# One instruction per convolution tap for latents and context, and GpSimd's arithmetic beside it on VectorE

## The chip, the cores and the metric

The kernel runs on one core of a Trainium2 chip. The metric is the device time of one execution in microseconds (us). A core has TensorE (matrix products), VectorE and ScalarE (elementwise work), GpSimd (elementwise work, and here the queue that issues part of the weight loads) and SyncE (which here only issues DMA). In the profile they are PE, DVE, ACT, POOL and SP; PEld is TensorE's load of weights. Each engine works through its own queue in order. L372 is line 372 of the kernel.

## The reference, cut to what matters

The model is a block with two linear-attention branches (gated delta rule, "GDN", and gated linear attention, "GLA") over 256 latent tokens and 256 context tokens, a routed mixture of 32 experts, and a second block behind it. The change lies in the inputs of the GDN branch: queries, keys and values go through a depthwise 3x3 convolution and a SiLU. The latents are an image of 4 rows of 64 tokens; the context is one row of 256 tokens, which sees the middle row of the taps only.

```python
def conv_latent(t, conv_w):
    b, l, ch = t.shape
    rows = l // GRID_W                      # 256 // 64 = 4
    return depthwise_conv2d(t.reshape(b, rows, GRID_W, ch), conv_w).reshape(b, l, ch)

def conv_context(t, conv_w):
    mid = CONV_SIZE // 2
    return depthwise_conv2d(t[:, None], conv_w[mid:mid + 1])[:, 0]

qkv_lat = jax.nn.silu(conv_latent(p_lat[..., :3 * GDN_WIDTH], conv_w))
qkv_ctx = jax.nn.silu(conv_context(p_ctx[..., :3 * GDN_WIDTH], conv_w))
```

Behind it, per head and direction, a chunked recurrence is solved: a triangular solve inside each chunk, then a scan over the chunks with a state of 128x128.

## The kernel before

Eight heads are worked in four pairs (gdn, L650). A generator, gdn_pair, holds the three steps of one pair. Its first step (L395 to L460) loads six blocks of w_in of 512 KB through GpSimd's queue (L399). It splits each into a high and a low part for exact fp32 products (wsplit, L381, with split, L48: the high part is rounded on ScalarE at L49, the low part is the difference at L50, on VectorE or, for the value blocks of the first two pairs, on GpSimd). It projects with three products for each of 8 blocks (mm3, L75), convolves (conv_silu, L357), transposes keys and values, and takes the norms with a reciprocal root (L57 to L72). The second step (L461 to L492) forms the decay matrices e, mt, at and qg. The third (L495 to L534) writes blocks of mt to DRAM, reads them back one block per partition (X), solves 31 steps of a triangular system on VectorE (L515, L516), and spreads the result with DMAs into AB. Then gdn_levels combines the blocks and gdn_scan runs the chunks.

In gdn the first pair's three steps come first. For each pair then the first step of the next pair is written, then levels and scan of this pair, then the other two steps of the next, then fill work that doesn't depend on them: lat_act (projections of gates), mod_steps (a modulation row, w_mod loaded through SyncE's queue into the same ring of six tiles as w_in, L161; TensorE product L162; a sum on VectorE at L172) and parts of the GLA branch. From this text the framework's planner sets the order of each engine's queue at build time by its own costs and inserts all waits; no order is written out by hand. So instructions of one pair run between those of another.

The convolution works on the transposed projection: 128 channels on the partitions, 256 (queries, latents only) or 512 tokens (keys and values: 256 latents, then 256 context) along the free dimension. ScalarE copies the latents into a zero-bordered pad of 6 rows of 66 (L364), starts the sum acc with the middle tap over all tokens (L365), and copies the context into a second pad of 258 (L367). Each of the eight other taps is one VectorE instruction over 256 latents, acc = pad x tap + acc (L372), rows outside the image included, where the pad is zero. For the two middle-row taps that the context has besides, ScalarE forms the product (L374, tile cx, one buffer) and GpSimd adds it (L375). A tanh (L377) and a closing product (L378) make the SiLU. There are 24 convolutions, 8 of them for queries.

Behind gdn come gla, merge, the expert stage (moe), whose weights stream through SyncE's queue, and the second block (post).

Of the kernel before, what the change touches and what calls it, by code (L numbers as in the profile page):

```python
# [7 lines left out]
F32 = mybir.dt.float32  # L8
# [4 lines left out]
OP = mybir.AluOpType  # L13
# [217 lines left out]
def gates(K, dbg=None):  # L231
# [4 lines left out]
    K.gdn_es = ExitStack()  # L236
    padp = K.gdn_es.enter_context(tc.tile_pool(name="pads", reuse_waits="tile", bufs=1, side="right"))
    for i in range(2):
        pl_ = padp.tile([P, 6, 66], F32, name=f"padl{i}")
        pc_ = padp.tile([P, 258], F32, name=f"padc{i}")  # L240
        nc.vector.memset(pl_, 0.0)
        nc.vector.memset(pc_, 0.0)
        K.pads.append((pl_, pc_))
    K.npad = 0
    es = ExitStack()
    gp = es.enter_context(tc.tile_pool(name="gp", reuse_waits="tile", bufs=1, side="right"))
# [110 lines left out]
def conv_silu(K, src, n_tok, ct, out, eng):  # L357

    nc = K.nc
    pl, pc = K.pads[K.npad % 2]  # L360
    K.npad += 1
    acc = K.gpool.tile([P, 512], F32, name="acc", bufs=2)
    al = acc[:, 0:256].rearrange("p (r w) -> p r w", r=4)
    nc.scalar.activation(pl[:, 1:5, 1:65], src[:, 0:256].rearrange("p (r w) -> p r w", r=4), AF.Copy)  # L364
    nc.scalar.activation(acc[:, :n_tok], src, AF.Copy, scale=K.taps[:, 4 * 24 + ct:4 * 24 + ct + 1])  # L365
    if n_tok > 256:
        nc.scalar.activation(pc[:, 1:257], src[:, 256:512], AF.Copy)  # L367
    cx = K.gpool.tile([P, 256], F32, name="cx")
    for tap in (0, 1, 2, 3, 5, 6, 7, 8):
        dy, dx = tap // 3, tap % 3  # L370
        w = K.taps[:, tap * 24 + ct:tap * 24 + ct + 1]
        eng.scalar_tensor_tensor(al, pl[:, dy:dy + 4, dx:dx + 64], w, al, op0=OP.mult, op1=OP.add)  # L372
        if n_tok > 256 and dy == 1:
            nc.scalar.activation(cx, pc[:, dx:dx + 256], AF.Copy, scale=w)  # L374
            nc.gpsimd.tensor_add(acc[:, 256:512], acc[:, 256:512], cx)  # L375
    th = K.gpool.tile([P, 512], F32, name="th", bufs=2)
    nc.scalar.activation(th[:, :n_tok], acc[:, :n_tok], AF.Tanh, scale=0.5)  # L377
    eng.scalar_tensor_tensor(out, th[:, :n_tok], 1.0, acc[:, :n_tok], op0=OP.add, op1=OP.mult)  # L378
# [12 lines left out]
def gdn_pair(K, pr):  # L391
# [14 lines left out]
    for hh in range(2):  # L406
        h = pr * 2 + hh
        H = Ctx()
        heads.append(H)
        H.h = h  # L410
        H.qT = gp.tile([P, 256], F32, name="qT", bufs=2)
        H.kT = gp.tile([P, 512], F32, name="kT", bufs=4)
        vT = gp.tile([P, 512], F32, name="vT", bufs=1)
        for j, (dst, n) in enumerate(((H.qT, 256), (H.kT, 512), (vT, 512))):

            hi, lo = wsplit(K, ws[hh * 3 + j], P, nc.gpsimd if pr < 2 and j == 2 else None)
            ps = psum.tile([P, 512], F32, name="pj", bufs=2)
            for k in range(8):
                mm3(nc, ps[:, :n], hi[:, k, :], lo[:, k, :], K.hh[:, k, :n], K.hl[:, k, :n], k == 0, k == 7)
            conv_silu(K, ps[:, :n], n, j * 8 + h, dst, nc.vector)  # L420

        pk = K.G()
        for t in range(4):
            nc.tensor.transpose(pk[:, t * P:(t + 1) * P], H.kT[:, t * P:(t + 1) * P], K.ident)
        H.kt = gp.tile([P, 4, P], F32, name="kt", bufs=4)
        nc.scalar.activation(H.kt, pk.rearrange("p (t n) -> p t n", t=4), AF.Copy)
        ns = gp.tile([P, 6], F32, name="ns", bufs=2)
        sq = gp.tile([P, 512], F32, name="th", bufs=2)
        for t in range(4):
            nc.scalar.activation(sq[:, t * P:(t + 1) * P], H.kt[:, t, :], AF.Square, accum_out=ns[:, t:t + 1])  # L430
        pn = K.G()
        sq = gp.tile([P, 512], F32, name="th", bufs=2)
        nc.scalar.activation(sq[:, :2 * P], H.qT, AF.Square)
        for t in range(2):
            nc.tensor.matmul(pn[:, t:t + 1], sq[:, t * P:(t + 1) * P], K.ones[:, 0:1], start=(t == 0), stop=(t == 1),
                             skip_group_check=True)
        nc.vector.tensor_copy(ns[:, 4:6], pn[:, 0:2])
        nq = gp.tile([P, 6], F32, name="nq", bufs=2)
        nc.vector.tensor_scalar(nq, ns, 4 * EPS, None, op0=OP.add)
        r = gp.tile([P, 6], F32, name="r", bufs=2)  # L440
        rsqrt(K, gp, r, nq, 6)

        r2 = gp.tile([P, 6], F32, name="r2", bufs=2)
        nc.vector.tensor_mul(r2, r, r)
        H.d = gp.tile([P, 2, 4], F32, name="d", bufs=4)
        bh = K.beta.rearrange("p d c h -> p d c h")[:, :, :, h]
        nc.vector.tensor_mul(H.d, bh, r2[:, None, 0:4].to_broadcast([P, 2, 4]))
        hn = gp.tile([P, 4], F32, name="hn", bufs=2)
        nc.vector.scalar_tensor_tensor(hn, nq[:, 0:4], 0.5, r[:, 0:4], op0=OP.mult, op1=OP.mult)
        nc.vector.tensor_scalar(K.aq[:, :, h], nq[:, 4:6], 128.0 * EPS, None, op0=OP.mult)  # L450

        pv = K.G()
        for t in range(4):
            nc.tensor.transpose(pv[:, t * P:(t + 1) * P], vT[:, t * P:(t + 1) * P], K.ident)
        H.vs = gp.tile([P, 4, P], F32, name="vs", bufs=4)
        for t in range(4):
            nc.scalar.activation(H.vs[:, t, :], pv[:, t * P:(t + 1) * P], AF.Copy, scale=hn[:, t:t + 1])
        H.dk = gp.tile([P, 2, 4], F32, name="dk", bufs=4)
        nc.vector.tensor_mul(H.dk, H.d, K.kds.rearrange("p (d t h) -> p d t h", d=2, t=4)[:, :, :, h])
    yield heads  # L460
    for hh, H in enumerate(heads):  # L461
# [14 lines left out]
        for d in range(2):  # L476
            gbc = gp.tile([P, 4, P], F32, name="gbc", bufs=2)
            nc.scalar.dma_start(gbc, dap(K.gD, d * 32 * P + h * P, [[0, P], [8 * P, 4], [1, P]]))
            e = gp.tile([P, 4, P], F32, name="e", bufs=2)
            s = 1 if d == 0 else -1  # L480
            nc.gpsimd.affine_select(out=e, in_=gbc, pattern=[[0, 4], [s, P]], compare_op=OP.is_ge,
                                    fill=-1e30, base=0, channel_multiplier=-s)
            for t in range(4):
                col = d * 32 + t * 8 + h
                nc.scalar.activation(e[:, t, :], e[:, t, :], AF.Exp, bias=K.ngc[:, col:col + 1])
            for t in range(4):
                nc.vector.scalar_tensor_tensor(H.mt[:, d, t, :], pg[:, t * P:(t + 1) * P], H.d[:, d, t:t + 1],
                                               e[:, t, :], op0=OP.mult, op1=OP.mult)
            nc.vector.tensor_mul(H.at[:, d], pq[:, 0:256].rearrange("p (t i) -> p t i", t=2), e[:, 0:2, :])
            nc.scalar.activation(H.qg[:, d], gbc[:, 0:2, :], AF.Exp)  # L490
            nc.gpsimd.tensor_mul(H.qg[:, d], H.qg[:, d], H.qT.rearrange("p (t i) -> p t i", t=2))
    yield  # L492


# [1517 lines left out]
```

## Time and profile before

| | us |
|---|---|
| median of 3 runs | 2082.15 (2078.74 to 2091.74) |
| profiled execution, its own time | 2083.65 |
| its span, first to last instruction | 2081.9 |
| TensorE busy | 1898.8 |
| VectorE busy | 965.6 |
| ScalarE busy | 652.5 |
| GpSimd busy | 184.0 |

The profile is of one execution. Busy is time in which an engine works on an instruction; idle time has a releaser, the instruction or DMA whose end let the engine go on. Groups of instructions show how many there are (xN), their busy time, the mean duration of one in ns, and the idle time before them. Durations by line are min/median/max in ns. PEclk is TensorE's granted clock as a share of full speed. The convolutions run from 66 to 407 us of the span, the expert stage from about 745 to 1710 us.

### The profile page before, as it was taken

Reading aid. Unit: us, or ns where it says so; the run is one execution under the profiler, and the core shown is the slowest. Engines: PE = TensorE matmul, PEld = TensorE weight load, DVE = VectorE, ACT = ScalarE, POOL = GpSimd, SP = SyncE. Lnnn points to the kernel's source line nnn. Section 1 sums busy time; section 2 is a strip of 40 time slices with the busy share of each in tenths; the row PEclk is TensorE's granted clock in tenths of the full one; section 3 lists DMA queues with packets and bytes.
Section 4 is the critical chain, followed back from the end, with each engine's and each line's share of the span. In section 5 each row is a group of like instructions: output and inputs, shape, how many; then the busy total and the mean of one; then the engine's idle time right before and its main releaser. Section 6 shows DMA issues by size and latency. Waiting matters only on the chain. (4 is left out here: it accounts for less than half of the span.)

```text
span 2081.9 us, 27700 instructions
## 1 busy us (share of the span) xinstructions
PE 1898.8 (91%) x10742; PEld 1159.6 (56%) x10743; DVE 965.6 (46%) x2245; ACT 652.5 (31%) x1369; POOL 184.0 (9%) x247
## 2 busy tenths in 40 slices
PE   4796989799998999999999999999999889989998
PEld 1664768687986763333333333333333228779997
DVE  2797785857464641212122221221211137676777
ACT  2553545467554420000000000000000004555554
POOL 1343122211112000000000000000000000000000
PEclk8798999899999989999999999999999988998999
DMA  7347654437544689999999999999999994433551
GB/s 261 77 122 206 183 169 116 112 103 206 169 151 151 254 325 417 417 414 418 417 416 418 418 416 417 418 416 417 418 418 416 417 345 139 140 102 121 183 182 41
DMA packets 191939, 569.60 MB, mean 274 GB/s; under 512 B 47919, under 2 KB 90776, under 8 KB 158650
## 3 DMA queue, kind: packets, MB, share of 16 engines
q1 hardware_dynamic: 160064, 507.19, 63.1%
q0 software_dynamic: 13392, 47.72, 7.4%
q10 hardware_dynamic: 18346, 12.86, 2.5%
q8 instruction: 86, 1.41, 0.3%
q14 instruction: 51, 0.42, 0.1%
HBM read 555.22 MB, written 12.50 MB: 273 GB/s over the span
## 5 line engine op out<-in xcount | busy, mean ns | idle before, releaser
L50 DVE TENSOR_TENSOR wlo<-w,whi 128x1024 fp32r<-128x1024 f32 (+1 forms) x185 | 223.9, 1211 | 132.6 <-ACT whi L49 129.8
L1308 PE MATMUL pg<-w,xT 128*64 128x512 f32 x1024 | 274.4, 605 | 3.5 <-DMA w<-in_w_gu_dram 3.4
L1308 PE MATMUL pl<-w,xT 128*64 128x512 f32 x1024 | 268.1, 593 | 0.0
L49 ACT ACTIVATE whi<-w 128x1024 fp32r<-128x1024 f32 (+1 forms) x189 | 197.3, 1047 | 217.8 <-PE pj L77 70.4
L1330 PE MATMUL po<-w,aT 128*64 128x512 f32 x1024 | 239.9, 608 | 7.1 <-DMA w<-in_w_down_dram 5.7
L1230 ACT ACTIVATE th<-ga 128x512 f32<-128x512 f32 x32 | 20.2, 632 | 613.8 <-DVE ga L1228 613.8
L1338 DVE TENSOR_TENSOR o<-po,g 64x512 f32<-64x512 f32 x64 | 44.1, 689 | 260.1 <-PE po L1330 259.4
L1308 PEld LDWEIGHTS pl<-w,xT 128*64 128x64 f32 x1024 | 75.2, 137 | 146.4 <-issue 146.4
L1330 PEld LDWEIGHTS po<-w,aT 128*64 128x64 f32 x1024 | 69.5, 139 | 141.7 <-issue 121.9
L1308 PEld LDWEIGHTS pg<-w,xT 128*64 128x64 f32 x1024 | 65.2, 136 | 139.4 <-issue 115.9
L1228 DVE TENSOR_SCALAR ga<-pg 128x512 f32<-128x512 f32 x32 | 22.1, 691 | 244.8 <-PE pg L1308 244.8
L77 PE MATMUL pj<-wlo,hh 128*128 128x256 f32 x384 | 116.2, 303 | 2.8 <-DVE wlo L50 2.8
L76 PE MATMUL pj<-whi,hh 128*128 128x256 f32 x384 | 115.2, 300 | 2.9 <-ACT whi L49 2.9
L78 PE MATMUL pj<-whi,hl 128*128 128x256 f32 x384 | 114.6, 299 | 0.0
L76 PE MATMUL pj<-hh,whi 128*128 128x512 f32 (+1 forms) x264 | 100.9, 384 | 12.6 <-ACT hh L49 9.1
L372 DVE SCALAR_TENSOR_TENSOR acc<-padl,taps,acc 128x256 f32<-128x256 f32 x192 | 104.3, 557 | 10.1 <-ACT acc L365 8.0
L78 PE MATMUL pj<-hh,wlo 128*128 128x512 f32 (+1 forms) x264 | 100.0, 380 | 5.9 <-DVE wlo L50 5.7
L77 PE MATMUL pj<-hl,whi 128*128 128x512 f32 (+1 forms) x264 | 100.9, 382 | 0.1
L1288 POOL CAST se<-sel 128x128 fp32r<-128x128 f32 x32 | 22.4, 702 | 828.4 <-PE pl L1292 828.4
L1267 PEld LDWEIGHTS tr<-S,h 128*128 128x128 f32 x480 | 57.9, 191 | 48.6 <-issue 34.9
L77 PEld LDWEIGHTS pj<-wlo,hh 128*128 128x128 f32 x384 | 78.0, 203 | 11.0 <-DVE wlo L50 4.2
L1360 PE MATMUL y<-o,PwT 128*128 128x512 f32 (+1 forms) x136 | 72.2, 641 | 13.0 <-DVE o L1338 10.2
(682 smaller groups left out, 3601.7 us busy)
## 6 DMA issues: line engine op xcount, KB each, us to landing
w<-in_w_gu_dram SPq DMA_DIRECT2D x256, 1024.0 KB, 18.2
w<-in_w_down_dram SPq DMA_DIRECT2D x139, 1024.0 KB, 20.0
w<-in_w_in_dram POOLq DMA_DIRECT2D x72, 512.0 KB, 5.4
w<-in_w_mod_dram SPq DMA_DIRECT2D x48, 512.0 KB, 6.9
w<-in_w_up_dram SPq DMA_DIRECT2D x22, 1024.0 KB, 5.1
w<-in_w_in_dram SPq DMA_DIRECT2D x8, 1024.0 KB, 9.8
gbc<-gD ACTq DMA_DIRECT2D x16, 256.0 KB, 6.2
actD<-la ACTq DMA_DIRECT2D x16, 256.0 KB, 5.0
```

Of the source, the lines that this page charges most:

```text
L49: K.nc.scalar.activation(hi, src, AF.Copy)
L50: (lo_eng or K.nc.vector).tensor_sub(lo, src, hi)
L76: nc.tensor.matmul(out, ah, bh, start=first, stop=False, **kw)
L77: nc.tensor.matmul(out, ah, bl, start=False, stop=False, **kw)
L78: nc.tensor.matmul(out, al, bh, start=False, stop=last, **kw)
L372: eng.scalar_tensor_tensor(al, pl[:, dy:dy + 4, dx:dx + 64], w, al, op0=OP.mult, op1=OP.add)
L1267: nc.tensor.matmul(p[:, kk * P:kk * P + m * CAP], h2[:, t, k * P:(k + 1) * P], S[:, t, e0:e1].rearrange("p e c -> p (e c)"), start=(kk == ...
L1288: nc.gpsimd.tensor_copy(se, sel[:, e, :, None].to_broadcast([P, 2, CAP]))
L1308: nc.tensor.matmul(pp[hs, :], xT[:, k, :], w[:, off + half * 512:off + half * 512 + 512], start=False, stop=(k == 7), skip_group_check=True)
L1330: nc.tensor.matmul(po[dh * CAP:(dh + 1) * CAP, :], aT[:, k % 4, (k // 4) * CAP:(k // 4 + 1) * CAP], w[:, kk * 1024 + dh * 512:kk * 1024 + ...
L1338: nc.vector.tensor_mul(outs[e // 2][e % 2 * CAP:(e % 2 + 1) * CAP, dh * 512:(dh + 1) * 512], po[hs], K.g2[hs])
L1360: nc.tensor.matmul(ps[dh], PwT[g][hs, t, :], outs[g][hs, dh * 512:(dh + 1) * 512], start=(g > 0), stop=True)
```

## The change

conv_silu gets one pad of 8 rows of 66 for latents and context. The context's 256 tokens are four more rows of 64. Since they are one row in truth, the last element of one of these rows and the first of the next are copied into each other's border (the tile view called ends: three pairs, one small ScalarE instruction). Each tap is then one VectorE instruction: taps of the middle row over all rows (8, or 4 for queries), taps of the upper row over latent rows 1 to 3, taps of the lower row over latent rows 0 to 2, as the rows left out have no neighbour there. ScalarE's products cx and GpSimd's sums are gone. The order of the taps is new. Two more pieces of GpSimd's arithmetic move to VectorE: the low half of the value blocks of the first two pairs, and the product for qg (16 of them).

```diff
     for i in range(2):
-        pl_ = padp.tile([P, 6, 66], F32, name=f"padl{i}")
-        pc_ = padp.tile([P, 258], F32, name=f"padc{i}")
-        nc.vector.memset(pl_, 0.0)
-        nc.vector.memset(pc_, 0.0)
-        K.pads.append((pl_, pc_))
+        pad = padp.tile([P, 8, 66], F32, name=f"pad{i}")
+        nc.vector.memset(pad, 0.0)
+        K.pads.append(pad)
...
 def conv_silu(K, src, n_tok, ct, out, eng):
-    pl, pc = K.pads[K.npad % 2]
+    pad = K.pads[K.npad % 2]
     K.npad += 1
+    n = n_tok // 64
     acc = K.gpool.tile([P, 512], F32, name="acc", bufs=2)
-    al = acc[:, 0:256].rearrange("p (r w) -> p r w", r=4)
-    nc.scalar.activation(pl[:, 1:5, 1:65], src[:, 0:256].rearrange("p (r w) -> p r w", r=4), AF.Copy)
+    av = acc.rearrange("p (r w) -> p r w", w=64)
+    nc.scalar.activation(pad[:, 0:n, 1:65], src.rearrange("p (r w) -> p r w", w=64), AF.Copy)
     nc.scalar.activation(acc[:, :n_tok], src, AF.Copy, scale=K.taps[:, 4 * 24 + ct:4 * 24 + ct + 1])
-    if n_tok > 256:
-        nc.scalar.activation(pc[:, 1:257], src[:, 256:512], AF.Copy)
-    cx = K.gpool.tile([P, 256], F32, name="cx")
-    for tap in (0, 1, 2, 3, 5, 6, 7, 8):
+    if n > 4:
+        ends = pad.rearrange("p r w -> p (r w)")[:, 4 * 66 + 65:4 * 66 + 65 + 3 * 66].rearrange("p (m e) -> p m e", e=66)
+        nc.scalar.activation(ends[:, :, 0:2], src[:, 319:511].rearrange("p (m e) -> p m e", e=64)[:, :, 0:2][:, :, ::-1], AF.Copy)
+    for tap in (1, 7, 3, 5, 0, 2, 6, 8):
         dy, dx = tap // 3, tap % 3
         w = K.taps[:, tap * 24 + ct:tap * 24 + ct + 1]
-        eng.scalar_tensor_tensor(al, pl[:, dy:dy + 4, dx:dx + 64], w, al, op0=OP.mult, op1=OP.add)
-        if n_tok > 256 and dy == 1:
-            nc.scalar.activation(cx, pc[:, dx:dx + 256], AF.Copy, scale=w)
-            nc.gpsimd.tensor_add(acc[:, 256:512], acc[:, 256:512], cx)
+        r0, r1 = ((1, 4), (0, n), (0, 3))[dy]
+        eng.scalar_tensor_tensor(av[:, r0:r1], pad[:, r0 + dy - 1:r1 + dy - 1, dx:dx + 64], w, av[:, r0:r1], op0=OP.mult,
+                                 op1=OP.add)
...
-            hi, lo = wsplit(K, ws[hh * 3 + j], P, nc.gpsimd if pr < 2 and j == 2 else None)
+            hi, lo = wsplit(K, ws[hh * 3 + j], P)
...
-            nc.gpsimd.tensor_mul(H.qg[:, d], H.qg[:, d], H.qT.rearrange("p (t i) -> p t i", t=2))
+            nc.vector.tensor_mul(H.qg[:, d], H.qg[:, d], H.qT.rearrange("p (t i) -> p t i", t=2))
```

## Rows read from the trace of the kernel before

**Rows 1.** The page, part 1: busy us, share of the span, instructions.

```profile
PE 1898.8 (91%) x10742; PEld 1159.6 (56%) x10743; DVE 965.6 (46%) x2245; ACT 652.5 (31%) x1369; POOL 184.0 (9%) x247
```

**Rows 2.** Busy time by stretch; last: granted clock, DMA share, GB/s.

```profile
core 0: us, PE busy (x) PEld busy (x) DVE busy (x) ACT busy (x) POOL busy (x), PEclk, DMA share, GB/s
62.00:170.00 108.00, 85.05 (x396) 64.79 (x394) 93.54 (x228) 61.36 (x159) 48.31 (x44) 0.86 0.44 110
...
222.00:305.00 83.00, 72.75 (x626) 52.28 (x625) 62.55 (x166) 44.15 (x109) 15.87 (x21) 0.96 0.51 155
305.00:396.00 91.00, 76.25 (x647) 66.39 (x645) 67.58 (x195) 47.99 (x118) 21.75 (x26) 0.89 0.44 114
396.00:495.00 99.00, 94.69 (x837) 86.08 (x838) 71.99 (x185) 67.69 (x132) 19.55 (x26) 0.91 0.54 146
...
745.00:1700.00 955.00, 902.76 (x4028) 332.94 (x4027) 199.32 (x355) 65.59 (x117) 22.36 (x31) 0.99 1.01 413
```

**Rows 3.** Groups of VectorE by form, 62 to 222 us: busy us, mean ns.

```profile
L372 DVE SCALAR_TENSOR_TENSOR acc<-padl,taps,acc 128x256 f32<-128x256 f32 x103 | 57.6, 586 | 2.4 <-ACT acc L365 1.6
L50 DVE TENSOR_TENSOR wlo<-w,whi 128x1024 fp32r<-128x1024 f32 x16 | 19.5, 1218 | 1.9 <-ACT whi L49 1.9
...
L72 DVE SCALAR_TENSOR_TENSOR r<-rs_a,r 128x6 f32<-128x6 f32 x12 | 3.6, 300 | 0.0
```

**Rows 4.** Groups of VectorE by form, 222 to 396 us.

```profile
L372 DVE SCALAR_TENSOR_TENSOR acc<-padl,taps,acc 128x256 f32<-128x256 f32 x82 | 42.4, 518 | 7.6 <-ACT acc L365 6.4
```

**Rows 5.** Durations by line on VectorE, whole span: min/median/max ns.

```profile
L372 DVE SCALAR_TENSOR_TENSOR acc<-padl,taps,acc x192: 468/484/2619, 77.3 to 405.5; 128x256 f32<-128x256 f32 x192
...
L72 DVE SCALAR_TENSOR_TENSOR r<-rs_a,r x24: 150/156/893, 107.9 to 414.3; 128x6 f32<-128x6 f32 x24
...
L378 DVE SCALAR_TENSOR_TENSOR qT<-th,acc x8: 412/426/969, 88.3 to 380.2; 128x256 f32<-128x256 f32 x8
L378 DVE SCALAR_TENSOR_TENSOR kT<-th,acc x8: 627/688/1074, 89.5 to 397.5; 128x512 f32<-128x512 f32 x8
```

**Rows 6.** Groups of GpSimd by form, 0 to 740 us.

```profile
L375 POOL TENSOR_TENSOR acc<-acc,cx 128x256 f32<-128x256 f32 x32 | 27.9, 872 | 80.9 <-ACT cx L374 76.9 <-DVE acc L372 4.0
...
L491 POOL TENSOR_TENSOR qg<-qg,qT 128x256 f32<-128x256 f32 x16 | 15.2, 954 | 16.2 <-ACT qg L490 13.4 <-DVE qT L378 2.3 <-DVE r L58 0.4
L50 POOL TENSOR_TENSOR wlo<-w,whi 128x1024 fp32r<-128x1024 f32 x4 | 12.3, 3070 | 6.4 <-ACT whi L49 6.2
```

**Rows 7.** Durations by line on ScalarE, whole span.

```profile
L364 ACT ACTIVATE padl<-pj x24: 361/367/392, 66.4 to 397.1; 128x256 f32<-128x256 f32 x24
...
L365 ACT ACTIVATE acc<-pj,taps x24: 454/673/713, 76.8 to 397.3; 128x512 f32<-128x512 f32 x16, 128x256 f32<-128x256 f32 x8
...
L374 ACT ACTIVATE cx<-padc,taps x32: 492/509/546, 78.8 to 401.4; 128x256 f32<-128x256 f32 x32
```

**Rows 8.** Timelines about 141 us, three engines: start, duration, [idle before, releaser].

```profile
138.22 4.70 POOL L50 TENSOR_TENSOR wlo<-w,whi 128x1024 fp32r<-128x1024 f32 x1 [4.87 <-ACT whi L49]
...
140.70 2.51 DVE L372 SCALAR_TENSOR_TENSOR acc<-padl,taps,acc 128x256 f32<-128x256 f32 x1
145.21 1.07 DVE L378 SCALAR_TENSOR_TENSOR kT<-th,acc 128x512 f32<-128x512 f32 x1 [2.00 <-ACT th L377]
...
143.84 0.51 ACT L374 ACTIVATE cx<-padc,taps 128x256 f32<-128x256 f32 x1 [5.30 <-POOL acc L375]
```

**Rows 9.** Waits, 0 to 420 us: total us, times, longest.

```profile
PE mod L162 <- DMA w<-in_w_mod_dram: 32.1, 12, 8.3
...
ACT cx L374 <- POOL acc L375: 14.1, 8, 5.3
...
DVE qT L378 <- ACT th L377: 10.0, 3, 5.8
...
DVE w L172 <- PE mod L162: 6.8, 1, 6.8
```

**Rows 10.** Durations of the solve's steps on VectorE, four pairs of 31.

```profile
L515 DVE TENSOR_TENSOR xtmp<-L,X x124: 161/327/901, 166.2 to 492.5; 128x112 f32<-128x112 f32 x8, 128x192 f32<-128x192 f32 x8, 128x240 f32<-128x240 f32 x8, 128x31 f32<-128x31 f32 x4
...
L516 DVE TENSOR_TENSOR X<-X,xtmp x124: 163/324/842, 168.0 to 493.3; 128x112 f32<-128x112 f32 x8, 128x192 f32<-128x192 f32 x8, 128x240 f32<-128x240 f32 x8, 128x31 f32<-128x31 f32 x4
```

## The prediction

> **What bounds the kernel now.** I read five views. First the page's busy times: TensorE carries the most [rows 1], but that is a mean over stages with different limits, so second, I cut the span into stretches [rows 2]. From 62 to 170 us, where the heads of the first two pairs go through the convolution, VectorE is busy for 93.54 of 108 us and TensorE for 85.05 at a granted clock of 0.86 (a mix of its two levels, 1.2 and 2.4 GHz): VectorE sets the pace. From 222 to 396 us no engine is full (VectorE 62.55 of 83, then 67.58 of 91; TensorE 72.75, then 76.25): chains of waits set the pace, and VectorE stands in most of them. From 396 us TensorE is full (94.69 of 99) with projections that wait in line, and from 745 to 1700 us the DMA engines are (share 1.01) with expert weights. So a microsecond gained before 396 us is kept: the filler work and then the weight loads begin that much earlier, and neither gets shorter. I count it one for one.
>
> Third, the groups of VectorE instructions and the durations by line. A tap (L372) takes 0.484 us at the median but 0.586 in the mean in the first stretch and 0.518 in the second [rows 3 to 5]. Fourth, the timelines say why: at 140.70 us one tap takes 2.51 us, and it ends 0.29 us behind GpSimd's low-half subtraction, which had run since 138.22 [rows 8]. VectorE is held while GpSimd reads SBUF. Behind the same GpSimd work ScalarE stood for 5.30 us before its next context product (L374), and VectorE then for 2.00 us for the tanh queued behind that product. The fifth view, who waits for whom, comes where a wait is priced.
>
> **The change, part by part.**
>
> *Holds that go.* GpSimd loses all three kinds of two-operand arithmetic: 32 context sums (L375), 16 products for qg (L491), 4 low halves (L50). The 103 taps of the first stretch lie 0.102 us above the median, 10.5 us; the 82 of the second 0.034, 2.8 us; the 12 last steps of the reciprocal root (L72) 0.144, 1.7 us [rows 3 to 5]. That is 15.0 us, a floor, since other instructions of the chain on SBUF operands (other root steps, closing products, solve steps) are held too and not counted. The ceiling is GpSimd's whole time in these groups, 27.9 + 15.2 + 12.3 = 55.4 us [rows 6]. I take 19, the floor and a quarter, because only what is near the floor is shown. GpSimd's mask (L481) stays, and its few holds with it.
>
> *Work that VectorE takes over.* Four low halves at 1.218 us are 4.9 us [rows 3]. Sixteen qg products of 128x256 on SBUF: the nearest row is the closing product of the same size, 0.426 us [rows 5], so 6.8 us.
>
> *The taps.* Every tap was 256 wide. Now, of eight, the two of the middle row take all rows (512 wide for keys and values, 256 for queries) and six take three rows (192 wide). No row shows either new width. The closing product (L378) goes from 0.426 us at 256 to 0.688 at 512 [rows 5], so 0.262 more for 256 columns and 0.0655 for 64: I take 0.484 + 0.262 = 0.746 us for the wide tap and 0.484 - 0.065 = 0.419 for the narrow. A key or value convolution then has 2 x 0.746 + 6 x 0.419 = 4.01 us of taps against 8 x 0.484 = 3.87, +0.13 each, 16 of them +2.1; a query convolution 0.97 + 2.51 = 3.48, -0.39 each, 8 of them -3.1. Sum -1.0. Bounds: a wide tap between 0.688 (no cost of rows) and 0.968 (two taps), a narrow one between 0.361 (0.426 - 0.065) and 0.484. That gives from 32 x 0.204 - 144 x 0.123 = -11.2 to 32 x 0.484 = +15.5 us.
>
> *ScalarE.* Per key or value convolution it loses two products with a tap (L374, 0.509 us each) and a 256-wide copy; the copy into the pad grows to 512 (0.673 at most, as L365's wide form, or twice 0.367), and a copy of six edge elements comes new, bounded by nothing and by that 0.367 [rows 7]. About 1 us less for each of 16. ScalarE isn't full, so I count none of it. If nothing hid it, the longer pad copy would delay a first tap by up to 0.37 us, 16 times, 5.9 us; the preceding convolution's taps, queued on VectorE, hide that.
>
> *Stalls that go.* The context product waited for GpSimd's sum 8 times, 14.1 us [rows 9]. In the case shown, 2.00 of 5.30 us reached VectorE [rows 8]; the same share of 14.1 is 5.3 us. Bounds: nothing, and the 10.0 us that VectorE spent waiting for tanh before a query's closing product [rows 9]. I take 5.3. What is late next is the tanh itself, behind the eight taps, as now.
>
> *Counted at nothing.* Two fills of zero pads for four: they run before 62 us, ahead of the first convolution's result. GpSimd's queue also issues the weight loads; it gets shorter by 55.4 us of work, yet the loads mostly wait for a free tile, not for GpSimd. If they did wait, this would be a gain more. No DMA is added or moved.
>
> Sum: -19 + 4.9 + 6.8 - 1.0 - 5.3 = -13.6 us. The profiled execution took 2083.65 us (span 2081.9), so 2070.0; the median of the runs, 2082.15, lies 1.5 lower, so **2069 us**.
>
> One rule of the Trainium skill speaks against the change: its page Perfetto Trace Analysis, section "Optimizing Scalar/DVE Operations", says that with a saturated VectorE it may make sense to move work to ScalarE or even to GpSimd; the change does the reverse where VectorE is the fullest. The section adds that the two share an SBUF read port, so that moving work between them might not help. By the first half alone the sum would be that of the third rival below; the held tap [rows 8] speaks for the second half.
>
> **The rivals.**
>
> *Given back at the modulation's loads.* TensorE waits 12 times, 32.1 us, for w_mod, and VectorE's L172 once, 6.8 us, for TensorE behind them, with solve steps queued after it [rows 9]. If these loads don't come sooner, what the first stretch gains is waited away there. For it: they are issued in order by SyncE and are paced by free tiles. Against: these tiles come free from low halves (L50), which come sooner. What is left is the second stretch: 3.5 us of holds, less half of the products, 3.4, and half of the stalls, 2.6: -2.7 us, so 2079.
>
> *TensorE speeds up too.* With its gaps closed, it would be granted the 0.96 of the stretch from 222 us also in the stretches at 0.86 and 0.89. That is 85.05 x (1 - 0.86/0.96) + 76.25 x (1 - 0.89/0.96) = 8.9 + 5.6 = 14.4 us more [rows 2], so 2054. Against: VectorE still sets the first stretch.
>
> *The moved work isn't paid for (slower).* Place: VectorE's queue, 62 to 396 us. If the holds fall on time in which VectorE would have waited anyway, their end gives nothing and the moved work stays: 4.9 + 6.8 - 1.0 = +10.7 us, so 2093. It decides below 10.7 us of holds returned. Against: the floor is 15.0, most of it where VectorE is 87% busy.
>
> *The solve falls behind the taps (slower).* The order of each queue is planned at build time, and new costs give a new order. A pair's solve is 31 products and 31 differences in a chain, 31 x (0.327 + 0.324) = 20.2 us [rows 10], now threaded between taps. If two of the four solves were put behind the next pair's taps and nothing else could run, +40.4 - 13.6 = +27 us: 2109. One alone ends at 2089; so it decides from two. Against: the order goes mostly by readiness in the trace before.
>
> **How the numbers follow.** My sum 0.52, given back 0.20, faster TensorE 0.12, moved work unpaid 0.08, solve behind 0.08. The sum's own range is 2058 to 2079: the taps' bounds (-10.2 and +16.5 about the value taken) with the stalls' (+5.3 and -4.7), neither likely at its end. The range for 8 in 10 reaches over the rival at 2079 and the one at 2093 and down to the middle of the faster TensorE: 2054 to 2093. One per cent is 20.8 us, about what a measurement of this kernel can tell from no change: below 2061 lie the faster TensorE and a quarter of my own case, 0.25; above 2103 the solve behind taps, 0.07; 0.68 between.
>
> **What would show it.** Right: taps of 512, 256 and 192 near 0.75, 0.48 and 0.42 us with means at their medians; no wait of ScalarE for GpSimd in the convolution; the last tap some 8 to 14 us earlier than 406 us and the expert stage begun by the same amount. Wrong: a wide tap near 0.97; VectorE's busy time before 396 us not lower; longer waits of L172 or L162; a solve that begins only behind the next pair's taps; or an expert stage that begins no earlier though the convolutions end sooner.

## The result and the profile after

The changed kernel takes 2098.8 us at the median (8 runs, 2089.7 to 2104.0), the kernel before beside it 2081.5 (8 runs, 2076.3 to 2091.7): a ratio of 1.0064, 95% interval 1.0040 to 1.0088, slower by about 13 us (the two medians lie 17 us apart; this text goes by the ratios). The prediction, 2069 us in a range of 2054 to 2093, was of a faster kernel. The profiled execution took 2098.73 us (span 2097.0).

The page's busy times first, against [rows 1]:

```profile
PE 1895.1 (90%) x10742; PEld 1153.3 (55%) x10743; DVE 948.5 (45%) x2263; ACT 641.0 (31%) x1337; POOL 132.6 (6%) x195
```

VectorE carries 17 us less although it has 18 instructions more, ScalarE 11.5 less, GpSimd 51 less. Work was taken off three engines, and the kernel got slower. The groups of VectorE by form, 62 to 222 us, against [rows 3] (busy us, mean ns):

```profile
L374 DVE SCALAR_TENSOR_TENSOR acc<-pad,taps,acc 128x192 f32<-128x192 f32 x72 | 27.7, 411 | 2.7 <-ACT acc L364 2.4
L374 DVE SCALAR_TENSOR_TENSOR acc<-pad,taps,acc 128x512 f32<-128x512 f32 x16 | 12.3, 768 | 0.0
L374 DVE SCALAR_TENSOR_TENSOR acc<-pad,taps,acc 128x256 f32<-128x256 f32 x8 | 3.8, 477 | 0.0
L490 DVE TENSOR_TENSOR qg<-qg,qT 128x256 f32<-128x256 f32 x8 | 3.3, 417 | 0.0
L72 DVE SCALAR_TENSOR_TENSOR r<-rs_a,r 128x6 f32<-128x6 f32 x12 | 1.9, 156 | 0.0
```

The holds are all but gone: the 256-wide tap has a mean of 477 ns where it had 586, the root's last step 156 where it had 300. Narrow and wide tap are 411 and 768 ns; one wide tap of 1.12 us lifts that mean, and from 222 to 396 us it is 745.

Where the time went shows in the stretches, against [rows 2] (us, PE busy, PEld, VectorE, ScalarE, GpSimd; then the granted clock, DMA share, GB/s):

```profile
62.00:170.00 108.00, 80.70 (x384) 58.55 (x382) 82.63 (x244) 53.06 (x138) 17.10 (x16) 0.87 0.45 120
...
305.00:396.00 91.00, 71.77 (x595) 61.42 (x594) 52.95 (x165) 40.38 (x99) 14.35 (x18) 0.78 0.44 124
396.00:495.00 99.00, 96.35 (x865) 87.33 (x864) 76.77 (x202) 66.09 (x131) 17.17 (x24) 0.98 0.50 135
```

In the first stretch VectorE falls from 93.54 to 82.63 of 108 us, and TensorE falls too, from 85.05 to 80.70. From 305 to 396 us TensorE is busy for 71.77 (76.25 before) at a granted clock of 0.78 (0.89). From 396 to 495 us the changed kernel does more than the one before (865 products for 837, clock 0.98 for 0.91), but that doesn't make up for it. The experts' first product by its line (durations in ns, first and last start), in the kernel before and then in the changed one:

```profile
L1308 PE MATMUL pg<-w,xT x1024: 592/592/1116, 759.9 to 1695.0; 128*64 128x512 f32 x171
```

```profile
L1307 PE MATMUL pg<-w,xT x1024: 592/592/1116, 778.4 to 1712.9; 128*64 128x512 f32 x171
```

And the stretch up to that start, again before and then changed:

```profile
0.00:759.90 759.90, 653.34 (x4554) 526.68 (x4555) 505.90 (x1353) 390.33 (x900) 158.29 (x211) 0.91 0.56 170
```

```profile
0.00:778.40 778.40, 653.88 (x4554) 523.66 (x4556) 488.91 (x1371) 378.64 (x868) 107.28 (x159) 0.90 0.53 166
```

From first to last start the experts take 935.1 and 934.5 us: that part is fixed. (Behind it some 3 us come back: the spans are 15.1 us apart.) Up to it TensorE has the same 4554 products and the same busy time, 653.3 and 653.9 us. Its idle time is 106.6 us before and 124.5 after: 18 us of idle time, and the experts begin 18.5 us later. So the question of this study is why TensorE idles more while VectorE has 17 us less to do.

Who waits for whom shows what differs. The longest waits of VectorE from 300 to 400 us (total, times, longest), in the kernel before and in the changed one:

```profile
DVE qT L378 <- ACT th L377: 6.7, 2, 5.8
DVE acc L372 <- ACT acc L365: 5.7, 2, 3.5
DVE ns L437 <- PE g L435: 3.5, 1, 3.5
```

```profile
DVE w L172 <- PE mod L162: 16.7, 1, 16.7
DVE la L685 <- ACT la L683: 10.6, 3, 9.6
DVE L L504 <- ACT L L503: 6.1, 1, 6.1
```

Before, VectorE waits for the parts of the convolution. After, it waits for the modulation's second sum (L172), for a latent projection's tanh (L683) and for the solve's first copy (L503): other instructions stand at the head of its queue when their inputs are late. Before, the second modulation sum ran at 304.0 us without a wait; the 6.8 us of L172 in [rows 9] were those of the first. No instruction of these three was changed. What changed is the order of the queues, which is planned at build time from the instructions' costs.

### The profile page after: what moved, and what is told of

Read it like the earlier page. It is cut to its first block, busy times and chain, and to the rows that moved or that the text cites. A ratio compares the mean times of both kernels' runs of the same rounds, so it can differ in the third digit from the quotient of the medians.

```text
span 2097.0 us, 27633 instructions
## 1 busy us (share of the span) xinstructions
PE 1895.1 (90%) x10742; PEld 1153.3 (55%) x10743; DVE 948.5 (45%) x2263; ACT 641.0 (31%) x1337; POOL 132.6 (6%) x195
## 5 line engine op out<-in xcount | busy, mean ns | idle before, releaser
L50 DVE TENSOR_TENSOR wlo<-w,whi 128x1024 fp32r<-128x1024 f32 (+1 forms) x189 | 228.2, 1208 | 142.2 <-ACT whi L49 139.4
L49 ACT ACTIVATE whi<-w 128x1024 fp32r<-128x1024 f32 (+1 forms) x189 | 197.3, 1047 | 262.2 <-PE pj L77 94.2
L374 DVE SCALAR_TENSOR_TENSOR acc<-pad,taps,acc 128x192 f32<-128x192 f32 (+2 forms) x192 | 87.4, 475 | 4.4 <-ACT acc L364 2.8
L162 PE MATMUL mod<-w,csP 128*32 128x512 f32 x192 | 56.6, 749 | 29.0 <-DMA w<-in_w_mod_dram 25.8
L1222 DVE TENSOR_TENSOR x<-x,y 128x512 f32<-128x512 f32 x68 | 46.5, 686 | 76.2 <-PE y L1359 76.2
```

The source lines that it names most:

```text
L49: K.nc.scalar.activation(hi, src, AF.Copy)
L50: (lo_eng or K.nc.vector).tensor_sub(lo, src, hi)
L162: nc.tensor.matmul(ps[32 * q:32 * q + 32, :], csP[:, k, :], w[:, q % 2 * 512:(q % 2 + 1) * 512], start=(k == 0), stop=(k == 7), skip_group ...
L374: eng.scalar_tensor_tensor(av[:, r0:r1], pad[:, r0 + dy - 1:r1 + dy - 1, dx:dx + 64], w, av[:, r0:r1], op0=OP.mult, op1=OP.add)
L1222: nc.vector.tensor_add(y[:, t, ds_], y[:, t, ds_], p)
```

## The experiments

The table gives for each kernel the median, the ratio to the kernel before on the same chip and its 95% interval.

| kernel | us | ratio | interval |
|---|---|---|---|
| changed kernel | 2098.8 | 1.0064 | 1.0040 to 1.0088 |
| e1: convolution alone | 2106.3 | 1.0102 | 1.0074 to 1.0130 |
| e2: moved work alone | 2083.5 | 0.9999 | 0.9978 to 1.0020 |
| e3: before, modulation steps late | 2139.2 | 1.0267 | 1.0224 to 1.0309 |
| e4: changed, modulation steps late | 2122.9 | 1.0189 | 1.0160 to 1.0218 |
| e5: before, half of the taps | 2107.8 | 1.0131 | 1.0094 to 1.0168 |
| e6: changed, second group earlier | 2104.6 | 1.0101 | 1.0069 to 1.0133 |
| e7: changed, store on ScalarE | 2095.1 | 1.0047 | 1.0026 to 1.0069 |
| e8: before, second group earlier | 2107.3 | 1.0115 | 1.0075 to 1.0155 |
| **e9: changed, in the order of before** | **2073.2** | **0.9936** | **0.9914 to 0.9957** |
| e10: before, in the changed order | 2106.4 | 1.0106 | 1.0076 to 1.0135 |
| e11: half of the taps, order of before | 2074.7 | 0.9945 | 0.9924 to 0.9966 |
| e12: convolution alone, order of before | 2072.8 | 0.9956 | 0.9933 to 0.9979 |
| e16: moved work alone, order of before | 2081.5 | 0.9979 | 0.9950 to 1.0008 |
| e13: changed, TensorE's order of before | 2084.9 | 1.0002 | 0.9980 to 1.0024 |
| e14: changed, VectorE's and ScalarE's | 2076.1 | 0.9955 | 0.9936 to 0.9974 |
| e15: changed, SyncE's and GpSimd's | 2092.1 | 1.0041 | 1.0018 to 1.0065 |
| e17: changed, VectorE's alone | 2088.0 | 1.0015 | 0.9996 to 1.0033 |
| e18: changed, ScalarE's alone | 2092.7 | 1.0048 | 1.0032 to 1.0064 |

The expectations of e1, e2 and e17 give numbers of taps that stand ahead of an instruction (121, 123, 103, 110; 81 and 74). These counts are wrong: equal neighbours in the queue had been counted once. Rightly counted, the second modulation sum stands behind 144 taps in both kernels, but behind 39 low halves in the changed one and 33 before (four of the six are those moved from GpSimd); the solves of pairs 0, 1 and 2 begin behind 88, 121 and 144 taps in the changed kernel and behind 94, 128 and 160 before. The new order puts the taps later against the solves, not earlier.

### Each part alone (e1, e2)

e1 is the changed kernel with the moved work undone; e2 is the kernel before with these two lines as in the changed one:

```diff
-            hi, lo = wsplit(K, ws[hh * 3 + j], P)
+            hi, lo = wsplit(K, ws[hh * 3 + j], P, nc.gpsimd if pr < 2 and j == 2 else None)
-            nc.vector.tensor_mul(H.qg[:, d], H.qg[:, d], H.qT...)
+            nc.gpsimd.tensor_mul(H.qg[:, d], H.qg[:, d], H.qT...)
```

> The convolution of the change; GpSimd keeps the low halves and the qg products. If the ends of the two modulation groups are what lost the time (theory A: cheaper VectorE work was never on the chain, and the new queue order puts the groups' last steps where they hold GpSimd's stores and the late weight loads), the time follows where those ends stand: here group 2's sum stands behind 121 taps as in the changed kernel (123; 103 before), so about 2090 to 2100. If the moved work is what costs (theory B), the merged taps alone give their gain: 2082 - 10 = 2070 or less. If the merged convolution itself costs (theory C), 2095 or more, and moves alone gain.

> The old convolution with the low halves and the qg products on VectorE. Theory A: group 2's sum stands behind 110 taps, between the two kernels, so between 2080 and 2095 without any relation to the 11.7 us of moved work. Theory B: 2082 + 10 to 17 = 2092 to 2099, all of the loss. Theory C: 2082 or below, since holds go and the convolution is the old one.

The convolution alone costs 21 us, the moved work alone nothing, and both together 13. The 8 us that are missing lie within the three intervals taken together, so this alone doesn't rule out a price per instruction. Taken by itself e1 speaks for theory C; e12 below shows that it was the order.

### The ends of the modulation groups (e3, e4, e6, e7, e8)

The first theory was that the second group's end, with its wait of 16.7 us on VectorE, its store on GpSimd and the weight loads queued behind that, carries the loss. e3 and e4 take the steps out of the stretch:

```diff
-    fill = [lat[0:1] + m1[0:3] + lat[1:2] + m1[3:6] + lat[2:3] + m1[6:8],
-            lat[3:4] + m2[0:3] + lat[4:5] + m2[3:6] + lat[5:6] + m2[6:8],
-            lat[6:10], lat[10:] + ...
+    fill = [lat[0:3],
+            lat[3:6],
+            lat[6:10], lat[10:] + m1 + m2 + ...
```

> The kernel before, with the 16 steps of modulation groups 1 and 2 moved out of the fillers of the first two pairs to the end of the last pair's filler, ahead of the gates. Their 33 us on TensorE leave a stretch with gaps and enter one that is full: 2082 + 10 to 33 = 2092 to 2115, unless the waits that they caused gave more than that. It is the partner of the next run.

> The changed kernel with the same steps moved in the same way. Theory A: with the groups' ends out of the stretch the change keeps its gain, so this one is 8 to 20 us below its partner (before with the steps moved), pair 3's convolutions end earlier than 408 us, and no store or weight load waits 20 us behind a sum. If the loss is somewhere else (theories B and C, or the solve's chain of DMAs), it stays about 15 us above its partner.

e3 is slower than expected (moving the steps costs the kernel before 56 us, not 10 to 33; it costs the changed one 26), and of these two the changed kernel is the faster one, by 16 us. That fitted theory A. It fits any theory by which a new order is drawn each time, and the next three runs bear on that. In e6 and e8 each block of the second group's steps is written ahead of its latent projection instead of behind it:

```diff
-            lat[3:4] + m2[0:3] + lat[4:5] + m2[3:6] + lat[5:6] + m2[6:8],
+            m2[0:3] + lat[3:4] + m2[3:6] + lat[4:5] + m2[6:8] + lat[5:6],
```

> The changed kernel with the second group's steps one filler earlier (each block of steps ahead of its projection instead of behind it); in the order of SyncE's queue the group's last weight load then stands ahead of pair 1's stores again, as in the kernel before. Theory A: the wait of 16.7 us on VectorE, that of 20.3 us on GpSimd and the late weight loads of pair 3 go, and the time comes to 2075 to 2088. If the end of the group isn't the cause: 2095 to 2105.

> The kernel before with the second group's steps one filler earlier: the partner of the changed kernel with that edit. Its group already ended at 304 us, ahead of pair 2's loads, so nothing is expected to move: 2078 to 2088. Theory A wants the changed kernel 5 to 15 us below this one; if the convolution itself costs (theory C), that one is 10 to 20 us above.

e7 only moves the store: `nc.scalar.dma_start(K.modD[g - 1]...)` in place of `nc.gpsimd`.

> The changed kernel with the store of each group's sum issued by ScalarE instead of GpSimd, so that pair 3's weight loads don't queue behind it; VectorE's own wait for the group's last product stays. If the queue behind the store is what carries the loss (theory A, its second half), 2082 to 2092; if VectorE's wait itself carries it, or neither does, 2095 to 2105.

By its own expectation theory A falls here. In e6 the sum starts at 314 us in place of 347 and its wait for TensorE is gone, and yet the kernel isn't faster (2104.6). VectorE's longest waits from 300 to 400 us in e6:

```profile
DVE la L685 <- ACT la L683: 16.2, 3, 14.8
DVE wlo L50 <- ACT whi L49: 9.3, 4, 4.6
DVE ns L436 <- PE g L434: 5.8, 2, 4.8
```

Another instruction stands at the head, for 14.8 us. But e6 has a newly planned order too: it shows that taking this wait away isn't enough, not what the wait cost. e8, the kernel before with one group one filler earlier and every instruction as it was, loses 24 us, more than the change does. e7 lies 4 us below the changed kernel by the ratios, less than the intervals tell from nothing.

### Less work on VectorE (e5)

```diff
-    for tap in (0, 1, 2, 3, 5, 6, 7, 8):
+    for tap in (1, 3, 5, 7):
```

> The kernel before with the four corner taps of every convolution left out (the output is another): 96 of 192 taps and their 52 us gone from VectorE's queue, nothing else. If VectorE sets the pace ahead of 396 us and a microsecond there is kept one for one, as the prediction has it, 2082 - 45 to 52 = 2030 to 2037. If other chains set it (the DMA round trips of the solve, the modulation's loads, the in-order queues) and VectorE's work fills what they leave, less than a third of it: 2065 to 2090.

VectorE has 39 us less to do up to the experts (466.8 us; 505.9 before), and the kernel is 27 us slower by the ratio. Neither expectation allowed for that. In its own new order VectorE's longest wait from 300 to 400 us is one of 16.1 us, of a low half (L50) for ScalarE's rounded copy (L49). This is the run that ended the argument from VectorE's busy time, and it made the order the suspect.

### The order held (e9 to e12, e16)

In these the order of every queue ahead of the experts is written out from the other kernel's built program. Each instruction of a queue gets an edge to the one before it that fixes their order of issue and adds no wait; instructions that only one kernel has stay free. In the traces, up to 740 us, the instructions of VectorE and ScalarE that both kernels have start in e9 in the order of before and in e10 in that of the changed kernel. The kernel before with its own order written out wasn't run, so a price of the edges by themselves isn't measured; e9 and e12, which have them, are faster than the kernel before, which hasn't.

```diff
+def pin(tc):
+    prog = tc.nc.cur_bb.bb.instructions
+    dep = mybir.DependencyInfo(mybir.DependencyClass.NoSync, mybir.DependencyReason.DATA)
...
+        for a, b in zip(ks, ks[1:]):            # ks: the queue in the other kernel's order
+            tc.add_manual_dep(q[b], q[a].name, dep, reason="pin")
...
         post(K)
+        pin(tc)
```

> The changed kernel with the order of every queue (TensorE, SyncE, VectorE, ScalarE, GpSimd, up to the experts) written out as that of the kernel before; only the 20 products and low halves that are new on VectorE are free to fall where they may. Order theory (the instructions of the change gain, and the newly planned order loses more than they gain): 2062 to 2076. Code theory (the merged taps and the moved work lose by themselves, whatever the order): 2092 to 2105. If neither order nor code matters alone: 2082.

> The mirror: the kernel before with every queue in the order of the changed kernel. Order theory: the loss comes with the order, 2098 to 2118 (the order's loss without the change's gain). Code theory: 2078 to 2088.

Both expectations of the order theory hold. By the ratios, with 2082 us for a ratio of one:

| | order of before | order of the changed kernel | cost of the order |
|---|---|---|---|
| instructions of before | 2082 | 2104 (+22) | 22 |
| instructions changed | 2069 (-13) | 2095 (+13) | 27 |
| gain of the instructions | 13 | 9 | |

The instructions gain in both orders (the 9 us are only just clear of the intervals); the order costs about twice what they gain. e9 is faster than both kernels. Its profiled execution took 2063.2 us, ten below its median, so its trace shows the gain too large. VectorE's longest waits from 300 to 400 us go with the order and not with the instructions, first e10 (old instructions, new order), then e9 (new instructions, old order):

```profile
DVE w L172 <- PE mod L162: 16.7, 1, 16.7
DVE la L686 <- ACT la L684: 11.8, 3, 10.8
DVE L L505 <- ACT L L504: 6.1, 1, 6.1
```

```profile
DVE qT L378 <- ACT th L377: 5.5, 2, 4.0
DVE acc L374 <- ACT acc L364: 5.4, 3, 3.3
DVE at L488 <- PE g L469: 3.9, 1, 3.9
```

e10 has the three waits of the changed kernel, to a tenth of a microsecond in two of them, without one changed instruction; e9 has the first two of before, at nearly their size. What TensorE did in the two stretches that differ most: before, changed, e9 and e10, one fence each (columns as above):

```profile
160.00:220.00 60.00, 43.64 (x260) 31.39 (x261) 44.67 (x138) 24.97 (x57) 15.87 (x20) 0.83 0.77 221
300.00:400.00 100.00, 82.94 (x688) 71.94 (x685) 72.91 (x208) 53.10 (x126) 26.52 (x33) 0.88 0.45 114
```

```profile
160.00:220.00 60.00, 44.60 (x242) 29.21 (x243) 41.86 (x133) 21.68 (x50) 13.63 (x16) 0.73 0.56 172
300.00:400.00 100.00, 80.52 (x639) 67.79 (x638) 58.69 (x194) 43.56 (x108) 14.90 (x20) 0.79 0.45 130
```

```profile
160.00:220.00 60.00, 50.41 (x319) 39.32 (x319) 44.59 (x131) 23.36 (x48) 12.73 (x17) 0.91 0.75 215
300.00:400.00 100.00, 89.52 (x809) 79.15 (x806) 73.72 (x214) 51.78 (x128) 12.39 (x18) 0.89 0.48 112
```

```profile
160.00:220.00 60.00, 39.78 (x225) 24.73 (x223) 46.56 (x142) 23.34 (x56) 18.72 (x22) 0.77 0.55 168
300.00:400.00 100.00, 75.94 (x608) 61.40 (x609) 58.67 (x177) 47.04 (x121) 21.20 (x26) 0.78 0.47 138
```

From 300 to 400 us the two kernels in the new order run 639 and 608 products, those in the old order 688 and 809. Busy time times granted clock, a rough measure of work done, is 73.0 before and 79.7 in e9 against 63.6 in the changed kernel and 59.2 in e10. The clock is lower besides: 0.78 and 0.79 in the new order, 0.88 and 0.89 in the old one. VectorE does less there too, 58.7 us in both against 72.9 and 73.7: a queue that stands at its head does none of its other work.

These waits of VectorE mark the order; that they are what it costs isn't shown, and two runs speak against it. In e2, which isn't slower, VectorE waits 10.4 us for a latent projection's tanh and 9.3 us at the second modulation sum, and pair 2's solve begins behind 144 taps, as in the changed kernel. In e8, which is 24 us slower, the second sum starts at 305.9 us without a wait, and VectorE's longest wait from 300 to 400 us is one of 6.7 us for a query's tanh. TensorE in the same stretch tells the two apart: 700 products at a clock of 0.85 in e2, 641 at 0.82 in e8 (e2 first):

```profile
300.00:400.00 100.00, 85.47 (x700) 73.17 (x698) 71.02 (x206) 53.34 (x126) 22.68 (x29) 0.85 0.45 122
300.00:400.00 100.00, 76.42 (x641) 66.33 (x642) 75.07 (x214) 51.95 (x134) 22.61 (x28) 0.82 0.43 107
```

> The kernel before without the four corner taps of each convolution (the output is another), in the order of the kernel before: the run without these taps in its own new order came to 2108. It prices 52 us of VectorE's work with the order held. If VectorE sets the pace ahead of 396 us and a microsecond is kept one for one: 2030 to 2040. If TensorE's waits for other things set it and only part reaches them: 2055 to 2078. If VectorE's work is free there: 2080 to 2085.

> The convolution of the change alone (GpSimd keeps low halves and qg products), in the order of the kernel before; in its own order it came to 2106. Order theory: below 2082, between 2066 and 2080, and the difference to the whole change in this order is the price of the moved work (0 to 12 us either way). Code theory: 2092 or more.

> The moved work alone (low halves and qg products on VectorE, the old convolution) in the order of the kernel before. If the moved work is unpaid, as the prediction's third rival has it: 2082 + 5 to 12 = 2087 to 2094. If the holds that go pay for it, as the prediction's sum has it: 2078 to 2085. If the whole gain of the change came from here and not from the convolution: 2070 to 2076.

With the order held, the parts add up: convolution 0.44% (9 us), moved work 0.21% (4 us, with nothing inside its interval), both 0.64% (13 us). The code theory of e12 is out: 2072.8 where it wanted 2092 or more. The moved work is not unpaid. e11 prices VectorE's work itself. Up to the experts VectorE has 39.7 us less to do than before (466.17 against 505.90), and the gain is 0.55%, 11.5 us. The stretch of e11 up to the experts' first product, which starts at 753.3 us:

```profile
0.00:753.30 753.30, 651.55 (x4556) 526.13 (x4557) 466.17 (x1257) 390.55 (x900) 154.88 (x211) 0.92 0.56 171
```

In the two profiled executions TensorE's idle time falls by 4.8 us and its busy time by 1.8, so the experts begin 6.6 us earlier. By the 11.5 us one microsecond of the taps is worth about 0.3, with the order held. e9 gives more, about 0.7: 13 us for 18.0 us less on VectorE (487.90 up to the experts), if all of its gain is put down to VectorE. So there is no one rate. The stretch of e9 up to the experts' first product:

```profile
0.00:740.80 740.80, 644.32 (x4556) 521.10 (x4557) 487.90 (x1371) 376.42 (x868) 103.12 (x159) 0.92 0.56 174
```

### Which queue's order (e13, e14, e15, e17, e18)

The changed kernel, with some of its queues in the order of before and the others planned anew around them.

> The changed kernel with TensorE's queue alone in the order of the kernel before; the other queues are planned anew around it. If the order of TensorE's products carries the loss, most of the 26 us between the two orders comes back: 2070 to 2082. If it is in the queues that issue DMAs or in VectorE's and ScalarE's, it stays at 2090 to 2105.

> The changed kernel with VectorE's and ScalarE's queues in the order of the kernel before, the rest planned anew. If these two carry the loss: 2070 to 2082, and the run with TensorE's order alone stays above 2090; if TensorE's does: 2090 or more. Both near 2075 would say that either fixes the other.

> The changed kernel with the two queues that issue most loads (SyncE and GpSimd) in the order of the kernel before, the rest planned anew. If a load or store queued in a bad place carries the loss (theory A's last form): 2070 to 2085. If not: 2090 to 2105.

> The changed kernel with VectorE's queue alone in the order of the kernel before. In the changed kernel's own order 81 taps and 15 low halves stand ahead of pair 0's solve (74 and 11 before), and 123 taps ahead of the end of pair 1's (103 before). If these taps pulled ahead of the solves carry the loss: 2068 to 2082, as with VectorE's and ScalarE's queues together (2076). If ScalarE's order does: 2088 or more.

> The changed kernel with ScalarE's queue alone in the order of the kernel before, the rest planned anew. If VectorE's order (taps ahead of the solves) carries the loss by itself: 2086 or more. If ScalarE's does: 2070 to 2082. Both near 2077: either holds the other, since ScalarE's copies and tanh stand in one chain with the taps.

VectorE's and ScalarE's queues together bring all but a few microseconds of what all five bring (2076 against 2073). Each of them alone doesn't: 2088 and 2093. e17 lies at the edge of what it expects if ScalarE's order carries the loss, and e18 contradicts that. TensorE's alone brings half (2085), between the two expectations of e13 and against that of e14, which wanted it above 2090; the two queues that issue most loads bring about a fifth by the ratios (2092). So the loss isn't in one queue: the taps on VectorE and the copies and tanh on ScalarE are one chain, and an order of one that the other doesn't share brings waits of its own. In e17 VectorE waits 21.4 us in all (12.6 at most) between 100 and 400 us for the tanh (L377) that ScalarE now has elsewhere.

What stays open is which few instructions out of place cost the 22 to 27 us. Taking away the wait of the modulation's sum isn't enough (e6), nor is moving its store (e7) or giving the loads their old order (e15). That the loss comes with the order is shown, and that in the changed kernel, e8 and e10 TensorE does less from 300 to 400 us (e15 and e18 are about 10 us slower than the kernel before without that: 723 and 700 products there). Of a single culprit nothing is shown.

## Why the prediction was wrong

**What VectorE's instructions cost: right, and more gained than forecast.** Wide tap 0.768 us in the first stretch and 0.745 in the second (0.746 taken), 256-wide 0.477 (0.484), narrow 0.411 (0.419), qg product 0.416 (0.426). VectorE's work up to the experts falls from 505.90 to 488.91, by 17.0 us; the sum had 8.3 (19 of holds and 1.0 of taps, less 4.9 and 6.8). The term that was too small is the holds: with taps at their new durations for 1.5 us less, 17.0 + 4.9 + 6.7 - 1.5 gives 27 us of them, between the floor of 15.0 and the ceiling of 55.4. That GpSimd's reads held VectorE is borne out: the longest time of the root's last step falls from 893 ns [rows 5] to 166, and in e10, which has GpSimd's old work in the new order, the longest tap takes 2.68 us again. The Trainium skill's page SBUF — State Buffer, section "Who interferes with whom", says that a VectorE instruction with two SBUF inputs contends with a GpSimd instruction that reads SBUF; these numbers agree.

**The stalls: those named are gone.** ScalarE's 14.1 us of waiting for GpSimd's sum [rows 9] are gone with the sum. VectorE's wait for tanh ahead of a query's closing product, 10.0 us, has no row among the longer waits any more; 5.3 us in two waits ahead of a value's are left.

**"VectorE sets the pace" and "I count it one for one": wrong.** This is the first step that failed. It was read from a busy share of 87% in the first stretch [rows 2], and a share says nothing of what a shorter queue would let begin. e11 gives 11.5 us for 39.7, e5 a loss for the same cut. What stays the same is the number of TensorE's products up to the experts. They keep it busy for 653.3 us before, 653.9 in the changed kernel, 651.6 in e11 and 644.3 in e9, and it is idle for 106.6, 124.5, 101.8 and 96.5. A microsecond elsewhere counts by what it takes from that idle time or from the time at a low clock. The sum of -13.6 is close to the 13 us that e9 shows, but by luck: it took half of VectorE's true saving and counted it one for one, where e11 returns 0.3 and e9 some 0.7 (0.5 to 1.0 by its interval), even if all of its gain is put down to VectorE. Its own range, 2058 to 2079, doesn't follow from the bounds that it names: with them, 2069 us reaches from 2054 to 2091, and the bounds of the holds were left out.

**The order of the queues: a rival at 0.08, and the whole result.** This is the step that decided. The prediction knew that "new costs give a new order" and put against it that "the order goes mostly by readiness in the trace before". It looked at one displacement only, a solve behind all of the next pair's taps, and asked for two of these before it decided. That form didn't come: pair 2's solve moved ahead of 16 taps, the other way. But the new order costs 22 us with the old instructions and 27 with the new. What would have told is an edit that changes no instruction: moving a group by one filler in the kernel before costs 24 us (e8). An edit of costs in this kernel is a new draw from such orders, and the prediction gave the draw no range. Of the orders planned anew in e1 to e8 none made a kernel faster than the one before.

**The other rivals.** *Given back at the modulation's loads*: not borne out. With the order held the gain is 13 us (e9) and not 2.7. In the changed kernel TensorE's products wait less for w_mod up to 420 us (25.8 us for 32.1), though its weight loads (PEld) wait more for it (44.0 for 40.4); the long wait of L172 comes with the order, since e10 has it with the old instructions. *TensorE speeds up too*: e9 has part of it, with granted clocks of 0.91 from 160 to 220 us (0.83 before) and 0.89 from 300 to 400 (0.88). The changed kernel has the reverse, 0.73 and 0.79. *The moved work isn't paid for*: out (e16). The rule of the Perfetto Trace Analysis page of the Trainium skill, by which a saturated VectorE would rather give work away, isn't borne out here either: giving VectorE 11.7 us of GpSimd's work costs nothing that e16 can tell. The part of that section on the shared port agrees with it.

**What would show it.** The list held in part. Of the signs named for wrong, a longer wait of L172 came (16.7 us behind TensorE's product, where the longest was 6.8, of another sum), and the expert stage begins no earlier, but the convolutions don't end sooner either, which that sign supposed. The signs named for right in the taps' durations and in ScalarE's wait came too, without a gain in time. The sign named for right, a last tap 8 to 14 us earlier than 406, came out as 419.2 in the changed kernel and as 385.8 in e9.

## What to carry to other kernels

Where the order of in-order queues is planned from costs, an edit has two prices: that of its instructions, and that of the new order. Measure the first with the order held, and the spread of the second by an edit that changes no instruction, before any sum; here the one was 13 us and the other over 20. To price a saved microsecond, don't go by the busy share of the fullest engine in a stretch: find the engine whose instructions up to the next fixed stage are the same in every version (here TensorE), and ask how much of its idle time, or of its time at a low clock, the saving can take away.

## What was not expected of the hardware

Half of the taps gone made the kernel 27 us slower in the order planned for it (e5) and 11.5 us faster in the old one (e11): 39 us from the order alone. In the changed kernel VectorE stood for 16.7 us at L172, and nothing else of its queue ran from 330.1 to 346.8 us; the Trainium skill's page Perfetto Trace Analysis, section "Tensor Engine Instruction (MATMUL, LD_WEIGHTS)", says that VectorE, ScalarE and GpSimd work strictly first in, first out, and the trace agrees. The copy of six edge elements, `L368`, takes 0.174 us at the median, against 0.576 for the pad copy of up to 512 columns (L363).
